# A convolution branch normalised in another place: standardise per token, scale and shift per channel on ACT, result kept in SBUF

## The chip, the core and the metric

One Trainium2 chip, and one of its cores. The kernel is a single program for the five engines of that core: PE (TensorE: matmuls and transposes), DVE (VectorE), ACT (ScalarE), POOL (GpSimd) and SP, whose queue issues most of the DMAs. The metric is device time in microseconds (us): the median of several runs of the whole program. A measurement of this kernel can tell about 0.2%, some 5 us, from no change.

## What is computed

One layer of a decoder with two kinds of heads, in float32, for 2048 tokens of width 1024. The part that matters here is the convolution group, one half of the mixer:

```python
def _layernorm(x, g, b):
    mu = jnp.mean(xf, axis=-1, keepdims=True)
    var = jnp.mean(jnp.square(xf - mu), axis=-1, keepdims=True)
    y = (xf - mu) * lax.rsqrt(var + EPS)
    return (y * g + b)

def _conformer_conv(val, gate, conv_w, conv_b, ln_g, ln_b):
    glu = val * jax.nn.sigmoid(gate)
    y = depthwise causal convolution of glu, width 31, 512 channels
    y = y + conv_b
    y = _layernorm(y, ln_g, ln_b)          # over the 512 channels of a token
    return jax.nn.silu(y)
...
a = _rmsnorm(h, g_pre_mix);  u = a @ w_in            # value, gate, q, k, v
attn_out = _rmsnorm(_stick_breaking(q, k, v), attn_norm_g)
y = concat(conv_out, attn_out) @ w_out
h = h + _rmsnorm(y, g_post_mix)
f = silu(_rmsnorm(h) @ w_gate) * (_rmsnorm(h) @ w_up) @ w_down
h = h + _rmsnorm(f, g_post_ffn)
```

## The kernel before

**Precision and layout.** Every dense product is done in three matmuls on numbers split into a high and a low part (H by a copy on ACT, L by a subtraction on DVE or POOL). Tokens go in four groups g of 512 (`G`), each of four tiles t of 128; 512 channels are four blocks c of 128. The convolution works with channels on the partitions and tokens along the free axis.

**Stages.** The mixer comes first: for each group the input projection (`inproj`), the taps of the convolution (`taps`), its normalisation (`convnorm`), attention in 128-query blocks (`attn`), and the output projection in two halves, `mixed`/`outproj` with part 0 for the convolution's channels and part 1 for attention's. The feed-forward follows, with seven products instead of eight per pair of blocks; its first piece, `c11`, and a second, `p4`, are run beside the last attention. PE alternates between these dense products and the small ones of attention.

**The convolution.** `taps(g)` accumulates 31 taps per channel block in the PSUM bank `cv`, one DVE instruction each (L817, L821), the last of which writes to `acc` in SBUF (one buffer). The bank `cv` exists once and serves, in the order in which it is asked for, the taps of the four blocks and then the transposes of `convnorm`; so the taps of group g+1 begin only when `convnorm(g)` has given it up.

**The normalisation.** `convnorm(g)` goes tile by tile. PE turns the tile to tokens on the partitions (`lps`, L834), ACT copies it to SBUF (L836), DVE makes mean and variance (L838, L840), POOL the inverse root (`rstd_of`, L537 and L538), DVE subtracts the mean and multiplies by the gain in one instruction and multiplies by the inverse root and adds the shift in another (L842, L843; gain `lng` and shift `lnb` are held broadcast over the partitions, 128x512 each), ACT makes the sigmoid (L845), POOL the product (L846), PE turns it back (`cps`, L851), ACT copies it (L853), and ACT's queue stores it to a scratch tensor `conv[g]` in DRAM (L854). Later `mixed(g, 0)` loads it block by block from SP's queue (L869) and splits it (L871, L872).

**What sets the order.** The mixer is first written down by generators that are advanced beside each other by the table `PLAN`. The instructions so recorded become a graph (`Graph`) with a cost of each instruction, buffers and links; `arrange` schedules it forwards and backwards several times and keeps the best, and `in_order` ties the instructions of each engine to that order. Any change of an instruction, a buffer or a dependency in the mixer may therefore move all the others. The feed-forward's order is pinned by hand, but for a few of its first instructions that may stand among the mixer's last. Tiles of `acc`, `cy`, `cs`, `lng`, `lnb` and others are used again as working space of the feed-forward (list `free`).

The steps of attention that are named later: `scores` makes z on PE (L908, L909), masks it on DVE (L911), takes two sigmoids on ACT (`om` L914, `A` L916), a running product on DVE (the scan, L918) and a product on POOL (`A`, L919); `values` turns A on PE (`at`, L935), splits it on ACT and DVE (`TH` L594, `TL` L595) and multiplies it with V (L940, L941). There are 320 scans in the mixer, and each engine's order can be counted by them.

## Time and profile before

| | |
|---|---|
| median of three runs | 2469.27 us (2466.63 to 2470.15) |
| the profiled execution | 2463.68 us, its span 2461.8 us |
| granted clock of PE | 0.993 of full speed |
| busy share PE, DVE, ACT, POOL | 96%, 73%, 52%, 62% |
| DMA | 657 MB, 267 GB/s on average |

The span is the time from the first to the last instruction of the profiled execution; its own time is 1.9 us longer. A row of a stretch gives, for each engine, busy time and number of instructions in it. "PEld" are the weight loads of PE, which overlap its matmuls. A matmul's record (about 390 ns for 512 columns) overlaps the next one's, so a stretch in which PE is "busy" all the time may still hold more matmuls than another. Instructions of DVE and ACT overlap a little as well.

### The profile page before, as it was taken

What the parts mean: (1) busy time and instruction counts of PE and PEld (TensorE: products, weight loads), DVE (VectorE), ACT (ScalarE), POOL (GpSimd) and SP (SyncE); (2) the same over time, 40 slices, a digit from 0 to 9 for tenths busy, and PEclk for the clock granted to TensorE, in tenths of its full rate; (3) what the DMA queues carried; (4) which work ended last, traced back from release to release, by engine and by line L of the source; (5) the groups of instructions that cost most, each with busy time, mean ns of one, the idle gap of its engine ahead of it and who ended that gap; (6) DMA issues with size and microseconds to landing.
All of it is one profiled execution on the core that took longest, in us unless ns stands there. A gap on an engine that the chain in (4) does not pass through costs nothing. (4 is left out here: it accounts for less than half of the span.)

```text
span 2461.8 us, 35571 instructions
## 1 busy us (share of the span) xinstructions
PE 2366.0 (96%) x11156; PEld 1927.0 (78%) x11156; DVE 1805.2 (73%) x2321; ACT 1290.2 (52%) x2398; POOL 1533.3 (62%) x1845
## 2 busy tenths in 40 slices
PE   8999999998999999999889998999999999999998
PEld 6788877786787878877678777787788887888886
DVE  6997999999997579998742247767665664557556
ACT  4557675685666566566654554333322334454543
POOL 5765567674667577659961138755656665568656
PEclk9999999999999999999999999999999999999999
DMA  9989876997689899976689768987878778658765
GB/s 324 290 304 287 259 235 218 300 310 250 226 263 307 277 330 325 324 261 202 201 299 312 252 256 294 319 280 257 295 273 291 258 246 282 196 190 273 248 190 178
DMA packets 289180, 657.31 MB, mean 267 GB/s; under 512 B 33888, under 2 KB 42080, under 8 KB 288992
## 3 DMA queue, kind: packets, MB, share of 16 engines
q1 hardware_dynamic: 264704, 622.01, 75.5%
q10 hardware_dynamic: 24288, 33.04, 3.7%
q8 instruction: 88, 1.44, 0.2%
q14 instruction: 100, 0.82, 0.1%
HBM read 460.92 MB, written 193.99 MB: 266 GB/s over the span
## 5 line engine op out<-in xcount | busy, mean ns | idle before, releaser
L919 POOL TENSOR_TENSOR A<-A,om 128x512 f32<-128x512 f32 (+2 forms) x320 | 326.2, 1021 | 286.1 <-DVE om L918 223.2
L1402 POOL TENSOR_TENSOR wL<-raw,wH 128x512 fp32r<-128x512 f32 x176 | 253.6, 1464 | 199.1 <-ACT wH L1401 168.2
L821 DVE SCALAR_TENSOR_TENSOR cv<-glu,cw,cv 128x512 f32<-128x512 f32 x464 | 345.7, 745 | 5.0
L1633 DVE TENSOR_TENSOR xL__22010<-t__22012,xH__22009 128x512 fp32r<-128x512 f32 x154 | 199.7, 1302 | 156.7 <-ACT xH__22009 L1632 155.1
L1631 POOL TENSOR_TENSOR xL__22008<-t__22011,xH__22007 128x512 fp32r<-128x512 f32 x154 | 211.4, 1380 | 153.2 <-ACT xH__22007 L1630 149.3
L918 DVE TENSOR_TENSOR_SCAN om<-om,one,z 128x513 f32<-128x513 f32 (+3 forms) x256 | 277.7, 1096 | 24.2 <-ACT A L916 21.9
L595 DVE TENSOR_TENSOR TL<-at,TH 128x512 fp32r<-128x512 f32 (+1 forms) x320 | 188.8, 600 | 105.5 <-ACT TH L594 79.2
L602 PE MATMUL inps<-xH,wL 128*128 128x512 f32 x640 | 257.8, 404 | 5.7 <-ACT sg L769 4.6
L606 PE MATMUL inps<-xL,wH 128*128 128x512 f32 x640 | 255.6, 400 | 0.0
L604 PE MATMUL inps<-xH,wH 128*128 128x512 f32 x640 | 254.4, 398 | 0.0
L914 ACT ACTIVATE om<-z 128x512 f32<-128x512 f32 (+2 forms) x320 | 173.7, 545 | 134.6 <-DVE z L911 67.5
L1108 PE MATMUL dps<-xH__22007,xL__22010 128*128 128x512 f32 x616 | 240.1, 390 | 2.5 <-DVE xL__22010 L1633 2.3
L1108 PE MATMUL dps<-xL__22008,xH__22009 128*128 128x512 f32 x616 | 240.1, 390 | 1.1 <-POOL xL__22008 L1631 1.0
L1108 PE MATMUL dps<-xH__22007,xH__22009 128*128 128x512 f32 x616 | 239.7, 389 | 0.0
L594 ACT ACTIVATE TH<-at 128x512 fp32r<-128x512 f32 (+1 forms) x320 | 169.3, 545 | 93.9 <-PE at L935 83.7
L935 PE MATMUL at<-idr,A 128*128 128x128 f32 x1088 | 200.7, 275 | 18.0 <-POOL A L919 9.4
L556 ACT ACTIVATE wH<-raw 128x1024 fp32r<-128x1024 f32 x156 | 166.3, 1066 | 89.2 <-PE inps L606 33.8
L1630 ACT ACTIVATE xH__22007<-t__22011 128x512 fp32r<-128x512 f32 x154 | 97.3, 632 | 214.7 <-POOL xL__22008 L1631 118.5
L1401 ACT ACTIVATE wH<-raw 128x512 fp32r<-128x512 f32 x176 | 101.2, 623 | 176.3 <-PE b L1108 53.2
L935 PEld LDWEIGHTS at<-idr,A 128*128 128x128 f32 x1088 | 140.6, 141 | 63.4 <-POOL A L919 16.0
L916 ACT ACTIVATE A<-z 128x512 f32<-128x512 f32 (+2 forms) x320 | 174.4, 549 | 4.3 <-PE at L935 3.6
L560 POOL TENSOR_TENSOR wL<-raw,wH 128x1024 fp32r<-128x1024 f32 x50 | 120.4, 2409 | 47.8 <-ACT wH L556 47.1
(304 smaller groups left out, 6347.9 us busy)
## 6 DMA issues: line engine op xcount, KB each, us to landing
wL<-wL SPq DMA_DIRECT2D x156, 512.0 KB, 5.5
raw<-in_w_in_dram SPq DMA_DIRECT2D x80, 512.0 KB, 5.7
t__22012<-u SPq DMA_DIRECT2D x154, 256.0 KB, 2.8
c<-c ACTq DMA_DIRECT2D x88, 256.0 KB, 5.7
t__22011<-wd SPq DMA_DIRECT2D x88, 256.0 KB, 2.9
K<-kd SPq DMA_DIRECT2D x80, 256.0 KB, 4.5
V<-vd SPq DMA_DIRECT2D x80, 256.0 KB, 4.6
u<-accf SPq DMA_DIRECT2D x22, 768.0 KB, 4.8
```

The lines of the kernel that those rows point to most:

```text
L595: nc.vector.tensor_tensor(L, ps, H.bitcast(F32), ALU.subtract)
L602: nc.tensor.matmul(ps, WL[:, kc], aH[t](k), start=k == 0, stop=False)
L604: nc.tensor.matmul(ps, WH[:, kc], aH[t](k), start=False, stop=False)
L606: nc.tensor.matmul(ps, WH[:, kc], aL[t](k), start=False, stop=k == KT - 1)
L821: nc.vector.scalar_tensor_tensor(to, gl[c][:, k:k + G], cw[:, c, k:k + 1], a, ALU.mult, ALU.add)
L918: nc.vector.tensor_tensor_scan(r, r, (one if late else z[:, 0:1]).to_broadcast([P, w + 1]), one, ALU.mult, ALU.bypass)
L919: nc.gpsimd.tensor_tensor(a[:, 0:w], a[:, 0:w], om[:, G - w + 1:G + 1], ALU.mult)
L935: nc.tensor.transpose(pt[:, j * P:(j + 1) * P], u["A"][j][:, b * P:(b + 1) * P], id32)
L1108: return nc.tensor.matmul(ps, a, b, skip_group_check=True, **flags)
L1402: nc.gpsimd.tensor_tensor(l, t, f32(h), sub)
L1631: nc.gpsimd.tensor_tensor(WL, w, f32(WH), sub)
L1633: nc.vector.tensor_tensor(UL, t, f32(UH), sub)
```

## The change

The gain and shift of the normalisation are moved from the turned tile, where they lie along the free axis, behind the second transpose, where they lie along the partitions.

- Per tile: ACT's copy of the turned tile goes back into the tile's own place in `acc`; the statistics read PSUM; one DVE instruction subtracts the mean and multiplies by the inverse root, in place.
- When the four tiles are done, per channel block: PE turns the 512 tokens back into the bank `cv`; ACT makes the sigmoid of scale x + shift into a rotating buffer (`ev`), and scale x + shift itself (Identity) into `acc`, with gain and shift as operands per partition; POOL multiplies the two in place.
- `acc` has two buffers and is handed to `mixed(g, 0)` as it is. The scratch tensor, its 16 stores from ACT's queue and its 16 loads from SP's queue are gone, as are `cy`, `cs` and the broadcast `lng` and `lnb`; the four small vectors (bias, attention's gain, gain, shift) are in one tile, the last two loaded in pieces of four bytes.
- The pauses between the steps (`LAG` times `yield 3` per tile) are half as long and stand behind each tile and each block.
- The working space of the feed-forward uses the second `acc` in place of the removed tiles.

```diff
-    lng = const(cc, "lng", ln_g.partition_broadcast(P), [P, CH])
-    lnb = const(cc, "lnb", ln_b.partition_broadcast(P), [P, CH])
-    ag = const(cc, "ag", attn_g, [P, CB])
+    small4 = cc.tile([P, 4, CB], F32, name="small4")
+    cb_, ag, lng, lnb = (small4[:, i, :] for i in range(4))
+    waiting += [(cb_, conv_b), (ag, attn_g)]
+    waiting += [(v, w.rearrange("(c p) -> p c", p=P)) for v, w in ((lng, ln_g), (lnb, ln_b))]
...
-        acc = vp.tile([P, CB, G], F32, tag="acc", name="acc", bufs=1)
-        conv[g] = dp.tile([P, CB, G], F32, name=f"conv{g}")
+        acc = conv[g] = vp.tile([P, CB, G], F32, tag="acc", name="acc", bufs=2)
...
-            ps = pp.tile([P, G], F32, tag="cv", name="lps", bufs=1)
+            ps = pp.tile([P, G], F32, tag="cv", name="lps", bufs=1).rearrange("p (c t) -> p c t", c=CB)
             for c in range(CB):
-                nc.tensor.transpose(ps[:, c * P:(c + 1) * P], acc[:, c, ts_], id32)
-            y = vp.tile([P, CH], F32, tag="cy", name="cy", bufs=1)
+                nc.tensor.transpose(ps[:, c, :], acc[:, c, ts_], id32)
+            y = acc[:, :, ts_]
             nc.scalar.activation(y, ps, AF.Copy)
             st = sp.tile([P, 6], F32, tag="st", name="st")
-            nc.vector.bn_stats(st, y)
+            nc.vector.bn_stats(st, ps.rearrange("p c t -> p (c t)"))
             mv = sp.tile([P, 3], F32, tag="mv", name="mv")
             nc.vector.bn_aggr(mv[:, 0:2], st)
             rstd_of(mv[:, 2:3], mv[:, 1:2], 1, "msc", 2)
-            nc.vector.scalar_tensor_tensor(y, y, mv[:, 0:1], lng, ALU.subtract, ALU.mult)
-            nc.vector.scalar_tensor_tensor(y, y, mv[:, 2:3], lnb, ALU.mult, ALU.add)
-            s = vp.tile([P, CH], F32, tag="cs", name="cs", bufs=1)
-            nc.scalar.activation(s, y, AF.Sigmoid)
-            nc.gpsimd.tensor_tensor(s, y, s, ALU.mult)
-            for _ in range(LAG):
+            nc.vector.tensor_scalar(y, y, mv[:, 0:1], mv[:, 2:3], ALU.subtract, ALU.mult)
+            for _ in range(LAG // 2):
                 yield 3
-            pt = pp.tile([P, G], F32, tag="cv", name="cps", bufs=1).rearrange("p (c t) -> p c t", c=CB)
-            for c in range(CB):
-                nc.tensor.transpose(pt[:, c, :], s[:, c * P:(c + 1) * P], id32)
-            r = s.rearrange("p (c t) -> p c t", c=CB)
-            nc.scalar.activation(r, pt, AF.Copy)
-            nc.scalar.dma_start(conv[g][:, :, ts_], r)
+        for c in range(CB):
+            ps = pp.tile([P, G], F32, tag="cv", name="cps", bufs=1)
+            for t in range(TT):
+                nc.tensor.transpose(ps[:, t * P:(t + 1) * P], acc[:, c, t * P:(t + 1) * P], id32)
+            s = ev("silu")
+            nc.scalar.activation(s, ps, AF.Sigmoid, scale=lng[:, c:c + 1], bias=lnb[:, c:c + 1])
+            nc.scalar.activation(acc[:, c, :], ps, AF.Identity, scale=lng[:, c:c + 1], bias=lnb[:, c:c + 1])
+            nc.gpsimd.tensor_tensor(acc[:, c, :], acc[:, c, :], s, ALU.mult)
+            for _ in range(LAG // 2):
+                yield 3
...
-        ms = [ma[g, p] if part else ev("m") for p in range(CB)]
-        if not part:
-            for k in range(CB):
-                nc.sync.dma_start(ms[k], conv[g][:, k, :])
+        ms = [ma[g, p] if part else conv[g][:, p, :] for p in range(CB)]
...
-        free = [t[:, 0:G] for t in gl] + [vp.tile([P, CH], F32, tag=n, name=n, bufs=1) for n in ("cy", "cs")]
-        acc = vp.tile([P, CB, G], F32, tag="acc", name="accf", bufs=1)
+        acc3, more = (vp.tile([P, CB, G], F32, tag="acc", name="accf", bufs=2) for _ in range(2))
```

The order of the mixer is made anew, and nearly every row of it moves. Three places matter. Lines behind L809 are numbered one to four lower after the change (L918 is L914, L821 is L820, L838 is L837).

DVE at the normalisation of group 1, before: the first of its four tiles, among scans (`om`) of attention.

```order
L838 BN_STATS st<-cy 128x6
L918 SCALAR_TENSOR_TENSOR om<-om,one,z 128x129
L840 BN_AGGR mv<-st 128x2
L918 SCALAR_TENSOR_TENSOR om<-om,one,z 128x257
L842 SCALAR_TENSOR_TENSOR cy<-cy,mv,lng 128x512
L911 TENSOR_TENSOR z<-z,msk 128x128 x2
L843 SCALAR_TENSOR_TENSOR cy<-cy,mv,lnb 128x512
```

The same place after:

```order
L837 BN_STATS st<-lps 128x6
L774 TENSOR_TENSOR glu_136<-inps,sg 128x512
L839 BN_AGGR mv<-st 128x2
L914 SCALAR_TENSOR_TENSOR om<-om,one,z 128x513
L841 TENSOR_SCALAR acc<-acc,mv 128x4x128
L837 BN_STATS st<-lps 128x6
```

The four tiles now stand within five scans of each other (behind scans 100 to 105), where they stood behind scans 96 to 123, and one instruction of 512 columns stands for two.

DVE at the first taps of group 3, before (`TL` is attention's split, `ot` and `ss` its own normalisation); 232 scans stand ahead of L817:

```order
L918 SCALAR_TENSOR_TENSOR om<-om,one,z 128x513
L963 TENSOR_REDUCE ss_11901<-sq 128x8
L817 TENSOR_SCALAR cv<-glu_137,cw,cbias 128x512
L595 TENSOR_TENSOR TL<-at,TH 128x256
L821 SCALAR_TENSOR_TENSOR cv<-glu_137,cw,cv 128x512
L918 SCALAR_TENSOR_TENSOR om<-om,one,z 128x513
```

After; 202 scans stand ahead of L816:

```order
L914 SCALAR_TENSOR_TENSOR om<-om,one,z 128x513
L816 TENSOR_SCALAR cv<-glu_134,cw,small_121 128x512
L820 SCALAR_TENSOR_TENSOR cv<-glu_134,cw,cv 128x512
L595 TENSOR_TENSOR TL<-at,TH 128x512
L914 SCALAR_TENSOR_TENSOR om<-om,one,z 128x513
L820 SCALAR_TENSOR_TENSOR cv<-glu_134,cw,cv 128x512 x2
```

The taps of group 3 begin 30 scans earlier; those of group 1 begin behind scan 48 instead of 50, those of group 2 behind scan 112 instead of 128.

ACT at the feed-forward's first Silu (`accf<-a`, L1416; `c` are the evictions of c11, L1149), before:

```order
L836 ACTIVATE cy<-lps 128x512
L1416 ACT_TABLE_LOAD
L1416 ACTIVATE accf<-a_17364 128x512
L594 ACTIVATE TH<-at 128x512
L916 ACT_TABLE_LOAD
L916 ACTIVATE A<-z 128x512
```

After:

```order
L1412 ACT_TABLE_LOAD
L1412 ACTIVATE accf<-a_17276 128x512
L1145 ACTIVATE c_15372<-c_15392 128x512
L1110 DMA c_2_1_0_0_15449<-c_15372 128x512
L556 ACTIVATE wH<-raw 128x1024
L1145 ACTIVATE c_15372<-c_15391 128x512
```

The Silu stands behind scan 309 of attention on ACT, where it stood behind scan 316; the load of the sigmoid's table that must follow it stands 13 rows further on. The feed-forward behind the mixer has the same rows in the same order as before on every engine.

More of the change, by code (lines that the diff above doesn't have):

```diff
@@ L631, in layer_kernel @@
     cw = const(cc, "cw", conv_w, [P, CB, CW])
-    cb_ = const(cc, "cbias", conv_b, [P, CB])
-    lng = const(cc, "lng", ln_g.partition_broadcast(P), [P, CH])
-    lnb = const(cc, "lnb", ln_b.partition_broadcast(P), [P, CH])
-    ag = const(cc, "ag", attn_g, [P, CB])
+    small4 = cc.tile([P, 4, CB], F32, name="small4")
+    cb_, ag, lng, lnb = (small4[:, i, :] for i in range(4))
+    waiting += [(cb_, conv_b), (ag, attn_g)]
+    waiting += [(v, w.rearrange("(c p) -> p c", p=P)) for v, w in ((lng, ln_g), (lnb, ln_b))]
     gpf = const(cc, "gpf", g_pre_ffn, [P, KT])
@@ L1352, in layer_kernel @@
         mixer.arrange()
-        free = [t[:, 0:G] for t in gl] + [vp.tile([P, CH], F32, tag=n, name=n, bufs=1) for n in ("cy", "cs")]
-        acc = vp.tile([P, CB, G], F32, tag="acc", name="accf", bufs=1)
-        sums3, us = acc[:, 0:3, :], four(acc)[0:3]
-        free += [acc[:, 3, :]]
+        acc3, more = (vp.tile([P, CB, G], F32, tag="acc", name="accf", bufs=2) for _ in range(2))
+        acc, more = four(acc3), four(more)
+        sums3, us = acc3[:, 0:3, :], acc[0:3]
+        free = [t[:, 0:G] for t in gl] + more[0:2] + [acc[3]]
         free += [fup.tile([P, G], F32, tag="rb", name="rbf")]
         free += [fup.tile([P, G], F32, tag="sum", name="sumf", bufs=3) for _ in range(3)]
-        free += [lng, lnb]
+        free += more[2:4]
         s1_, u_ = cycle(free[0:2]), cycle(free[3:6])
```

## The prediction

> **What bounds the kernel now.** I read the page first (busy time by engine), then the busy time of each engine by stretches of the span, then the waits inside the stretches in which TensorE (PE) loses time, and last the rows of the lines that the change touches.
>
> ```profile
> span 2461.8 us, 35571 instructions
> PE 2366.0 (96%) x11156; PEld 1927.0 (78%) x11156; DVE 1805.2 (73%) x2321; ACT 1290.2 (52%) x2398; POOL 1533.3 (62%) x1845
> ...
> core 0: us, PE busy (x) PEld busy (x) DVE busy (x) ACT busy (x) POOL busy (x), PEclk, DMA share, GB/s
> 180.00:250.00 70.00, 69.95 (x380) 57.53 (x379) 53.13 (x87) 50.72 (x102) 40.76 (x87) 1.00 0.91 289
> 250.00:460.00 210.00, 199.93 (x1004) 162.86 (x1004) 206.44 (x304) 126.69 (x245) 131.70 (x206) 1.00 0.76 248
> 460.00:540.00 80.00, 79.64 (x429) 64.40 (x428) 73.18 (x106) 66.87 (x138) 64.72 (x127) 1.00 0.92 302
> 540.00:740.00 200.00, 190.62 (x931) 150.82 (x931) 196.87 (x289) 119.53 (x227) 116.95 (x201) 0.99 0.77 250
> 740.00:940.00 200.00, 196.97 (x1018) 160.84 (x1017) 143.29 (x190) 133.09 (x253) 142.01 (x216) 1.00 0.91 307
> 940.00:1140.00 200.00, 195.26 (x947) 159.45 (x946) 192.07 (x252) 119.98 (x221) 131.49 (x173) 0.99 0.83 285
> 1140.00:1310.00 170.00, 152.28 (x738) 121.80 (x737) 98.15 (x116) 105.58 (x200) 129.94 (x169) 0.96 0.74 253
> 1460.00:2461.00 1001.00, 968.24 (x4252) 794.39 (x4250) 646.42 (x676) 394.67 (x716) 644.01 (x479) 1.00 0.75 253
> 2250.00:2430.00 180.00, 179.87 (x794) 148.55 (x793) 108.59 (x93) 87.87 (x165) 113.22 (x86) 1.00 0.71 228
> ```
>
> PE is busy for 96% of the span, so nothing can be won but PE's idle time, and that lies unevenly. In 250 to 460 us PE loses 210 - 199.9 = 10.1 us and in 540 to 740 us 9.4 us, and in both VectorE (DVE) is busy for 98% (206.4 of 210, 196.9 of 200). These are the stretches in which DVE runs the convolution's taps of groups 1 and 2 beside attention. Between them, in 460 to 540 us, where group 1 is normalised, DVE has 6.8 us free and PE loses 0.4 us. In 740 to 940 us, while group 2 is normalised, DVE has 57 us free; the taps of group 3 follow in 940 to 1140 us (DVE 96%, PE loses 4.7 us). From 1460 us on the feed-forward runs; the order of its instructions is unchanged on every engine. So I look at the mixer, and there at DVE.
>
> ```profile
> PE z L908 <- DVE om L918: 6.3, 10, 1.1
> PE ops L1034 <- DVE big L1039: 3.7, 2, 3.3
> PE o L941 <- DVE TL L595: 3.0, 6, 1.0
> PE o L940 <- ACT TH L594: 2.4, 4, 0.9
> ```
>
> These are PE's waits in 250 to 760 us (total, times, longest): 13.0 us of the longest four end on DVE, 2.4 us on ACT. DVE's queue is in order, so whatever leaves it lets the scans and splits that PE waits for come sooner.
>
> **What the change takes from DVE.** The rows have count, busy time and mean of one in ns:
>
> ```profile
> L843 DVE SCALAR_TENSOR_TENSOR cy<-cy,mv,lnb 128x512 f32<-128x512 f32 x16 | 16.8, 1052 | 8.9 <-POOL mv L538 8.9
> L842 DVE SCALAR_TENSOR_TENSOR cy<-cy,mv,lng 128x512 f32<-128x512 f32 x16 | 15.0, 937 | 0.3
> L838 DVE BATCH_NORM_STATS2 st<-cy 128x6 f32<-128x512 f32 x16 | 10.9, 684 | 0.6 <-ACT cy L836 0.6
> L719 DVE TENSOR_SCALAR hrow<-hrow,rstd 128x1024 f32<-128x1024 f32 x12 | 9.9, 821 | 1.8 <-POOL rstd L538 1.8
> L817 DVE TENSOR_SCALAR cv<-glu,cw,cbias 128x512 f32<-128x512 f32 x16 | 12.9, 806 | 0.3
> ```
>
> For each of the 16 token tiles two scalar_tensor_tensor go (937 + 1052 = 1989 ns) and one tensor_scalar of 128x512 comes. No row has it in this shape. Upwards it is bounded by L817, 806 ns (two scalars per partition, but into PSUM); downwards by half of L719, 410 ns (SBUF to SBUF, one scalar, twice as wide). I take 450 ns, near the second, because source and target are both in SBUF as there. The statistics read PSUM instead of SBUF; I leave them at 684 ns. So a tile gives DVE 1989 - 450 = 1.54 us (bounds 1.18 and 1.58), a group of four tiles 6.2 us, all sixteen 24.6 us. Only what falls in or next to the two full stretches counts.
>
> *Group 1 (540 to 740 us).* Its four tiles stand at 460 to 540 us. The 6.2 us saved there and the 6.8 us that DVE has free there are 13.0 us into which taps of group 2 can move up. By the order they do: the first tap of group 2 stands behind scan 112 of attention on DVE, and stood behind scan 128.
>
> ```profile
> 0.00:500.00 500.00, 112.00 (x112) 1.00 0.85 277
> 0.00:820.00 820.00, 211.86 (x200) 1.00 0.84 276
> 0.00:962.00 962.00, 259.19 (x241) 1.00 0.85 281
> ```
>
> (Scans L918 begun so far; the number behind x counts them.) Scan 112 comes at 500 us. With 13.0 us less, DVE is at 184 of 200 us in this stretch and no longer full, and PE's 190.6 us of work become the limit: at most 9.4 us. What PE still loses beside a DVE at 92 to 96% lies between 0.4 us in 80 us (460 to 540 us, that is 1.0 in 200) and 4.7 us in 200, so the gain is 4.7 to 8.4 us. I take 6.5 us; the ends are 0 (if PE is held by something else) and 9.4 us.
>
> *Group 0 (250 to 460 us).* Its four tiles stand at 190 to 250 us, where DVE is not full (53 of 70 us) and PE loses nothing. The saving helps the full stretch behind only as far as taps of group 1 begin earlier: they stand behind scan 48 instead of 50, two scans, some 3 us of DVE work. I take 3 us, between 0 and the 6.2 us saved.
>
> *Group 2 (740 to 1140 us).* Its own saving is worth nothing: DVE has 57 us free there, which cover it. But its chain is shorter (below), so the taps of group 3 begin behind scan 202 instead of 232, at about 820 us. By scan 240 some 70 more taps have been issued than before, 70 x 0.745 = 52 us of DVE work moved from the stretch behind 940 us to the one ahead of it.
>
> ```profile
> L821 DVE SCALAR_TENSOR_TENSOR cv<-glu,cw,cv 128x512 f32<-128x512 f32 x464 | 345.7, 745 | 5.0
> ```
>
> PE loses 3.0 + 4.7 = 7.7 us in the two stretches now. In 740 to 962 us, where scan 240 began, DVE had 143.3 + 0.96 x 22 = 164 us of work; with 52 more and 6.2 saved it is 210 of 222 us, 95%, between the 92% of 460 to 540 us (1.0 lost in 200) and the 96% of 940 to 1140 us (4.7 in 200): some 4 us lost. The 178 us behind it are left with DVE at about 67%, as in 740 to 940 us (3.0 in 200): 2.7 us lost. So 6.8 instead of 7.7 us; I take 1 us of gain. The ends are a gain of 4.7 us, and the loss that the second rival prices.
>
> *Group 3.* Its tiles stand behind 1180 us, where DVE is at 58% or less. Nothing.
>
> **What the change does on ACT, POOL, PE and the queues.**
>
> ```profile
> L845 ACT ACTIVATE cs<-cy 128x512 f32<-128x512 f32 x16 | 10.4, 649 | 5.4 <-DVE cy L843 3.8 <-DMA conv<-cs 1.6
> L836 ACT ACTIVATE cy<-lps 128x512 f32<-128x512 f32 x16 | 9.9, 620 | 7.7 <-PE lps L834 7.6
> L853 ACT ACTIVATE cs<-cps 128x512 f32<-128x512 f32 x16 | 9.8, 614 | 1.6 <-PE cps L851 0.9 <-POOL pv L921 0.6
> L975 ACT ACTIVATE ma<-po,ag 128x512 f32<-128x512 f32 x16 | 11.0, 689 | 5.4 <-PE po L973 5.4
> L854 ACTq DMA_DIRECT2D conv<-cs x16: 520/521/587, 205.3 to 1381.0; - x16
> L869 SPq DMA_DIRECT2D m<-conv x16: 371/440/1519, 339.5 to 1393.0; - x16
> conv<-cs ACTq DMA_DIRECT2D x16, 256.0 KB, 6.4
> m<-conv SPq DMA_DIRECT2D x16, 256.0 KB, 5.7
> ```
>
> ACT keeps three ACTIVATEs per tile, but two of them now take scale and bias per partition. One such operand costs 689 - 614 = 75 ns (L975 against L853), so two make 764 ns; 620 + 2 x 764 = 2148 ns stand for 649 + 620 + 614 = 1883 ns, 4.2 us more in all. Against that ACT no longer issues 16 stores (16 x 0.52 = 8.3 us of its queue) and SP no longer issues 16 loads (16 x 0.44 = 7.0 us). ACT gains 4 us, which is worth nothing where it is 60% busy. The 8 MB of traffic (of 657 MB) and the two landings of 6.4 and 5.7 us leave the way from the convolution to its projection; the first store is issued at 205 us and the first load at 339 us, and for the last group PE had c11 to do meanwhile, so that cover makes it worth nothing too. POOL keeps its 16 products and PE its 128 transposes: no change.
>
> The Trainium skill speaks against this placement: its page "ScalarE: Activation LUTs", section "Rules for kernel authors", sends multiply and add to VectorE, not to ScalarE. By that rule scale and shift would cost DVE another 806 ns (L817) per channel block, the saving per group would fall from 6.2 to 3.0 us, and the sum to about half. The stretches above decide against the rule here: DVE is 98% busy where ACT is at 60%.
>
> The chain of waits through the one PSUM bank `cv` gets shorter. Before, each tile went through transpose, copy, statistics, POOL, two DVE steps, sigmoid, POOL and back, eight steps in line, before the next tile had the bank; now the bank is free when copy and statistics have read it (0.62 and 0.68 us). The bank then goes to the four channel blocks, each held for two ACTIVATEs (1.5 us). That, not the DVE time alone, lets the next taps start 16 and 30 scans earlier.
>
> At the start, two loads of 256 KB (gain and shift, broadcast) become two of 2 KB in pieces of four bytes. Nearest rows:
>
> ```profile
> L513 SPq DMA_DIRECT2D cbias<-in_conv_b_dram x1: 708/708/708, 4.7 to 4.7; - x1
> L513 SPq DMA_DIRECT2D lng<-in_conv_ln_g_dram x1: 328/328/328, 7.6 to 7.6; - x1
> ```
>
> With four times as many pieces as cbias each takes SP between 0.33 and 4 x 0.71 = 2.8 us; behind them stands the third weight load. I take 0, ends -0.5 and +2 us.
>
> Last, the feed-forward's first Silu moves. It had to wait for the single `acc`; with two it takes group 2's and stands on ACT behind scan 309 instead of 316, among the first evictions of the second half of c11.
>
> ```profile
> 1370.13 1.28 ACT L1416 ACT_TABLE_LOAD   x1
> ...
> 1372.57 1.28 ACT L916 ACT_TABLE_LOAD   x1
> ...
> 1378.53 0.50 PE L1108 MATMUL c<-xH,wL 128*128 128x512 f32 x1 [2.35 <-ACT c L1149]
> ...
> L1462 SPq DMA_DIRECT2D a<-c x2: 319/372/426, 1268.5 to 1274.9; - x2
> ...
> DMA to landing us min/median/max: 5.8/6.5/7.1
> ```
>
> The two table loads (1.28 us each) remain. Behind them PE waited 2.35 us; at the new place ACT could also wait for the Silu's operand, whose load was issued at 1268.5 us and takes 6.5 us. I take 0 (the same stall elsewhere), ends -2.4 and +6 us.
>
> **Sum.** -6.5 - 3 - 1 + 0 + 0 = -10.5 us. The profiled execution took 2463.68 us (span 2461.8 and 1.9 us around it), so 2453.2 us, 0.43% less. The three runs have a median of 2469.27 us, 0.23% above that execution; 0.43% off the median is 2459 us. Differences under 0.2% (4.9 us) a measurement of this kernel can hardly tell from none.
>
> **Rivals.**
>
> *More than that.* If PE's real room is larger than its idle time, DVE's relief is the limit: 6.2 + 13.0 us. The weight loads (PEld) speak for it: where PE runs without a gap, in 2250 to 2430 us, they are busy 148.55 of 180 us, 82.5%; in the two full stretches 77.6% and 75.4%, which leaves 210 - 162.86/0.825 = 12.6 and 17.2 us, not 10.1 and 9.4. Then -20 us, about 2449 us. Against it: attention's chains and the two PSUM banks of the projections also hold PE. The Trainium skill says the same of the measure ("Perfetto Trace Analysis", section "Identifying the Most-Contended Engine": judge TensorE by LDWEIGHTS busy, not by matmul busy); the trace agrees, as these shares show.
>
> *The gain is given back.* The taps pulled ahead fill DVE from 740 us on. Should DVE be as full over 740 to 1040 us as it was in 540 to 740 us, PE loses 9.4/200 x 300 = 14.1 us there instead of 3.0 + 2.4 = 5.4, that is +8.7 us, and the sum is -9.5 + 8.7 = -0.8 us: 2468 us, no difference. For it: the 95% worked out above are not far from 98%. Against it: at 96% PE lost half as much. It decides at a DVE share of 98% in that stretch.
>
> *Slower.* ACT stops at the Silu behind scan 309: its operand's load shares SP's queue with weight loads that wait for their own buffers. While ACT stands, c11 can fill two banks of 12 matmuls (24 x 0.227 = 5.4 us, by the 794 in 180 us of 2250 to 2430 us), then PE stops, and attention with it. A stall of S costs S + 2.6 - 5.4 - 2.4; to turn -10.5 us into a loss of 5 us it must be 21 us. Against it: that load took 6.5 us. At S = 25 us the time is about 2474 us.
>
> **How the numbers follow.** The forecast 0.50, more 0.14, given back 0.22, slower 0.14. Faster is the first two, 0.64. The forecast's own range is 2454 to 2464 us. To leave out no more than two in ten I reach to 2447 us (most of the second case) and to 2473 us (the third whole, the slower one in part).
>
> **What would show it.** Right: DVE below 95% and PE's loss below 4 us in 540 to 740 us; the taps of group 3 from about 820 us; tensor_scalar near 0.45 us; the span from 1460 us on, counted from the projection's end, unchanged. Wrong: DVE at 98% in 740 to 1040 us; a gap on PE of more than 5 us behind an ACT_TABLE_LOAD; tensor_scalar at 0.8 us; or new PE waits in 1140 to 1310 us, where it loses 17.7 us already and where the order has moved as well.

## The result, and the profile after

| | before | after |
|---|---|---|
| median of 4 runs, us | 2469.71 (2466.63 to 2471.67) | 2448.31 (2442.64 to 2451.81) |
| profiled execution, us (span) | 2463.68 (2461.8) | 2447.04 (2445.3) |

The ratio is 0.9911, 95% interval 0.9893 to 0.9930: the changed kernel is 0.89% faster, some 22 us. The direction is as forecast and the time lies inside the range, but the gain is twice the 0.43% that the sum gave. The two profiled executions differ by 16.6 us. They ran at the same granted clock of PE, 0.993; the four executions of the changed kernel had 0.992 to 0.994, those of the kernel before 0.986 to 0.994 in the experiments below, 0.990 on average. In the last set its executions at 0.986 to 0.988 took 2470.4 to 2473.1 us, and those at 0.992 and 0.993 took 2463.2 to 2466.5 us, some 7 us for 0.005; by this estimate some 4 us of the 22 go with the clock, and why the two kernels get different ones stays open.

First the page's line of busy time by engine, and the stretches of the changed kernel (per stretch: length, then busy time with count of PE, PEld, DVE, ACT, POOL, the granted clock, DMA share, GB/s):

```profile
span 2445.3 us, 35497 instructions
...
PE 2360.7 (97%) x11156; PEld 1927.7 (79%) x11156; DVE 1786.1 (73%) x2305; ACT 1295.6 (53%) x2398; POOL 1528.3 (62%) x1845
```
```profile
250.00:460.00 210.00, 208.00 (x1052) 171.36 (x1051) 207.45 (x315) 132.23 (x255) 135.69 (x218) 1.00 0.79 254
460.00:540.00 80.00, 77.33 (x410) 62.67 (x409) 76.62 (x110) 67.08 (x133) 61.16 (x123) 0.98 0.87 287
540.00:740.00 200.00, 195.46 (x972) 157.50 (x972) 196.24 (x286) 126.44 (x239) 125.66 (x216) 0.99 0.78 255
740.00:940.00 200.00, 194.34 (x1000) 157.76 (x999) 173.68 (x238) 130.36 (x244) 134.87 (x205) 1.00 0.91 308
940.00:1140.00 200.00, 194.04 (x942) 157.06 (x940) 151.47 (x190) 123.44 (x229) 136.34 (x175) 1.00 0.80 267
1140.00:1310.00 170.00, 153.65 (x753) 123.61 (x752) 95.50 (x110) 104.32 (x193) 118.58 (x160) 0.98 0.75 256
```

In 250 to 460 us PE loses 2.0 us where it lost 10.1, in 540 to 740 us 4.5 instead of 9.4. In both, DVE is as full as before (207.45 of 210, 196.24 of 200). In 740 to 1140 us PE loses more than before, 11.6 instead of 7.8 us. All in all the span is 16.5 us shorter. PE's idle time fell from 95.8 to 84.6 us (span less busy), that is 11.2 of it; the other 5.3 us are busy time of the same 11156 matmuls (2366.0 to 2360.7), which the forecast did not count at all. In the last 1001.8 us of the span PE is busy for 968.2 us before and 968.3 us after: the feed-forward is unchanged, as forecast.

DVE is full and PE runs: what changed is what DVE is full of. The taps' line alone in 540 to 740 us, before and then after:

```profile
540.00:740.00 200.00, 87.43 (x119) 0.99 0.77 250
```
```profile
540.00:740.00 200.00, 75.75 (x102) 0.99 0.78 255
```

The 124 operations of a group's taps took from 537 to 740 us, nearly the whole stretch; now they go from 490 to 726 us. In this stretch that is 17 taps and 11.7 us fewer. Attention's scans, splits (`TL`) and masks got only 2.7 us of the place, the first tiles of group 2's normalisation 3.2 us, and projections and smaller pieces the rest; but what PE waits for comes sooner. The waits of PE in 250 to 760 us (total, times, longest) show it: the four longest rows were 15.4 us together, and are 6.5 us now.

```profile
PE z L904 <- DVE om L914: 3.0, 3, 1.7
PE ops L1030 <- DVE xL L868: 1.3, 1, 1.3
PE po L969 <- DVE ot L961: 1.3, 1, 1.3
PE o L936 <- ACT TH L594: 0.9, 2, 0.8
```

The rows of the lines that are new (min/median/max ns, first and last start):

```profile
L841 DVE TENSOR_SCALAR acc<-acc,mv x16: 515/548/1623, 194.7 to 1220.7; 128x512 f32<-128x512 f32 x16
L837 DVE BATCH_NORM_STATS2 st<-lps x16: 667/696/700, 191.2 to 1213.9; 128x6 f32<-128x512 f32 x16
L849 ACT ACTIVATE silu<-cps,small x16: 774/820/869, 213.3 to 1383.6; 128x512 f32<-128x512 f32 x16
L850 ACT ACTIVATE acc<-cps,small x16: 779/819/876, 214.0 to 1384.3; 128x512 f32<-128x512 f32 x16
```

### The profile page after: what moved, and what is told of

Read it like the earlier page. It is cut to its first block, busy times and chain, and to the rows that moved or that the text cites. A ratio compares the mean times of both kernels' runs of the same rounds, so it can differ in the third digit from the quotient of the medians.

```text
span 2445.3 us, 35497 instructions
## 1 busy us (share of the span) xinstructions
PE 2360.7 (97%) x11156; PEld 1927.7 (79%) x11156; DVE 1786.1 (73%) x2305; ACT 1295.6 (53%) x2398; POOL 1528.3 (62%) x1845
## 5 line engine op out<-in xcount | busy, mean ns | idle before, releaser
L820 DVE SCALAR_TENSOR_TENSOR cv<-glu,cw,cv 128x512 f32<-128x512 f32 x464 | 346.8, 747 | 4.7
L914 DVE TENSOR_TENSOR_SCAN om<-om,one,z 128x513 f32<-128x513 f32 (+3 forms) x256 | 278.3, 1100 | 16.6 <-ACT A L912 13.6
L931 PEld LDWEIGHTS at<-idr,A 128*128 128x128 f32 x1088 | 140.1, 140 | 58.2 <-POOL A L915 16.5
```

The costliest lines, as they stand in the source:

```text
L820: nc.vector.scalar_tensor_tensor(to, gl[c][:, k:k + G], cw[:, c, k:k + 1], a, ALU.mult, ALU.add)
L914: nc.vector.tensor_tensor_scan(r, r, (one if late else z[:, 0:1]).to_broadcast([P, w + 1]), one, ALU.mult, ALU.bypass)
L931: nc.tensor.transpose(pt[:, j * P:(j + 1) * P], u["A"][j][:, b * P:(b + 1) * P], id32)
```

## The experiments

Eighteen kernels, each timed in five rounds against the kernel before. The theories: **D**, DVE's work that leaves is the gain (the forecast's step). **P** (called C or "the chain" in the expectations), the new path through the bank `cv` (statistics from the bank, all four tiles first, then the four channel blocks, two `acc` tiles) is the gain, by an earlier and more even start of the next taps. **M**, the round trip through DRAM. **O**, the planner, given other work, happened to find a better order. In the edits, lines are cut to what differs.

### First set: putting single parts back

**dve_back**

```diff
-nc.vector.tensor_scalar(y, y, mv[:, 0:1], mv[:, 2:3], ALU.subtract, ALU.mult)
+nc.vector.scalar_tensor_tensor(y, y, mv[:, 0:1], idb, ALU.subtract, ALU.mult)
+nc.vector.scalar_tensor_tensor(y, y, mv[:, 2:3], idb, ALU.mult, ALU.add)
```

> The changed kernel with the two DVE instructions per tile put back: two scalar_tensor_tensor of 128x512 with a constant tile as second operand stand for the one tensor_scalar; the values are therefore not the normalised ones. The rest (statistics from PSUM, bank cv given back early, result kept in SBUF) is as in the changed kernel. Theory D (the gain is DVE work that left the two full stretches): the 1.4 us per tile come back, 6 us before the taps of group 1 and 6 before those of group 2, 2460 to 2466 us. Theory C (the gain is the shorter chain through the bank cv, which lets taps begin earlier): 2448 to 2453 us. Theory M (the DRAM round trip) and theory O (the order is new and happens to be good): no statement that tells them apart here.

Measured: 2454.69 us (2453.35 to 2456.67), ratio 0.9944 (0.9932 to 0.9956). DVE has all its old work again, and two thirds of the gain stay: D is not the whole gain.

**dve_less**, the other side, in the kernel before:

```diff
-nc.vector.scalar_tensor_tensor(y, y, mv[:, 0:1], lng, ALU.subtract, ALU.mult)
-nc.vector.scalar_tensor_tensor(y, y, mv[:, 2:3], lnb, ALU.mult, ALU.add)
+nc.vector.tensor_scalar(y, y, mv[:, 0:1], mv[:, 2:3], ALU.subtract, ALU.mult)
```

> The kernel before with only its two scalar_tensor_tensor per tile replaced by one tensor_scalar (subtract the mean, multiply by the inverse root); gain and shift are left out, all else (tile by tile through the bank cv, store to DRAM and load) is as before. Theory D: most of the gain, 2451 to 2458 us. Theory C: next to none, 2464 to 2470 us. Theory M: none, 2466 to 2471 us.

Measured: 2472.64 us (2467.59 to 2483.88), ratio 1.0021 (1.0007 to 1.0034). With the old path and in this order, the relief of DVE gains nothing: in the full stretches DVE is a little emptier (206.4 and 196.9 us before), but the weight loads, PE's work, are as before (162.86 and 150.82 us). The relief was smaller than meant, too: the sixteen tensor_scalar took 960 ns on average. And the granted clock is lower in this execution (0.99 and 0.97 here, 1.00 and 0.99 before).

```profile
250.00:460.00 210.00, 202.44 (x1000) 162.84 (x999) 200.49 (x296) 129.09 (x246) 141.16 (x213) 0.99 0.77 252
540.00:740.00 200.00, 193.20 (x925) 151.82 (x923) 194.00 (x283) 121.40 (x226) 120.47 (x200) 0.97 0.80 252
```

**dram_back**

```diff
+nc.scalar.dma_start(conv[g][:, c, :], acc[:, c, :])
-ms = [ma[g, p] if part else conv[g][:, p, :] for p in range(CB)]
+ms = [ma[g, p] if part else ev("m") for p in range(CB)]
+nc.sync.dma_start(ms[k], conv[g][:, k, :])      # four per group
```

> The changed kernel with the round trip put back: ACT's queue stores each finished channel block to DRAM (16 stores of 256 KB) and SP's queue loads it ahead of the split (16 loads). Theory M (8 MB of traffic, 16 issues on ACT's and 16 on SP's queue, and the two landings were worth something): 2453 to 2460 us. Theories D and C: 2447 to 2451 us, as the changed kernel.

Measured: 2455.54 us (2452.51 to 2458.05), ratio 0.9946 (0.9934 to 0.9958).

**after_hop**, the changed kernel with `HOP = 63.0` in place of `60.0`, a cost that only the planner uses:

> The changed kernel with one number of the planner's cost model changed (the hop after a wait 63 for 60 ns): same instructions, another order of the mixer. Theory O: the order alone moves the time by 5 us and more, anywhere from 2440 to 2460 us. Theories D, C and M: within 4 us of the changed kernel, 2444 to 2452 us.

Measured: 2450.55 us (2445.76 to 2455.14), ratio 0.9931 (0.9918 to 0.9944).

### Second set: both parts back, and the old order of tiles

**both_back** is dve_back and dram_back together.

> The changed kernel with the two scalar_tensor_tensor per token tile on DVE and the round trip of the convolution's result through DRAM both put back (the constant tile of the second steps makes the normalised values wrong); the path of the tiles through the bank cv is the changed kernel's. The first taps of groups 2 and 3 stand behind scans 107 and 202. If DVE's work or the traffic carries the gain, nothing of it is left: 2466 to 2471 us. If the shorter path through the bank, which lets the taps begin earlier, carries it: faster than the kernel before by 7 to 13 us, 2456 to 2462 us. If it is only a lucky order of the changed kernel (scatter of the planner), anything from 2455 to 2475 us.

Measured: 2460.54 us (2455.48 to 2466.71), ratio 0.9973 (0.9962 to 0.9984). All of the old DVE work and the old round trip, on the new path: still 7 us faster than before.

**tile_by_tile**

```diff
+            for _ in range(LAG):
+                yield 3
+            pt = (bank cv) ... four transposes of this tile
+            nc.scalar.activation(s, pt, AF.Sigmoid, ...); Identity; product on POOL
-        for c in range(CB): ...        # the loop over channel blocks
```

> The changed kernel (one tensor_scalar per tile, result stays in SBUF) but each token tile goes through the bank cv to the end before the next one enters, as in the kernel before; scale and shift take channel block 0's operands for all blocks (left out: the right gain and shift of blocks 1 to 3). The first taps of groups 2 and 3 stand behind scans 116 and 205, near the changed kernel's 112 and 202. If the early start of the taps carries the gain: 2448 to 2455 us. If it is the order by channel blocks itself (four long holds instead of four tiles): 2460 us or more. DVE's work and the traffic, as theories of their own, say 2448 us too, so this run tells only about the order by blocks.

Measured: 2459.40 us (2451.94 to 2461.59), ratio 0.9962 (0.9948 to 0.9976). About half of the gain is left, in one order of this work. The edit also puts the pause per tile back to its old length.

**before_lag3** is the kernel before with `LAG = 3`.

> The kernel before with LAG = 3 instead of 4 (the planner's pause between the two transposes of a tile), and nothing else: same instructions, same DVE work, same DRAM round trip. The first taps of groups 2 and 3 move up from scans 128 and 232 to 118 and 218. If an early start of the taps carries the gain: 2459 to 2464 us, some two thirds of the way in scans giving about half of the gain. If DVE's work or the traffic carries it: within 2 us of the kernel before, 2467 to 2472 us. If the planner's orders scatter by more than that: no theory is helped.

Measured: 2469.41 us (2461.83 to 2473.44), ratio 1.0011 (0.9998 to 1.0023): no gain. Its stretches 540 to 740 and 1140 to 1310 us:

```profile
540.00:740.00 200.00, 193.06 (x953) 154.13 (x952) 197.38 (x283) 127.45 (x241) 122.05 (x211) 0.99 0.78 258
1140.00:1310.00 170.00, 145.65 (x699) 114.44 (x697) 99.96 (x106) 99.82 (x190) 129.12 (x162) 0.96 0.71 240
```

The earlier taps do what P says where they run (PE loses 6.9 us instead of 9.4), and the later stretch takes it back (24.3 us instead of 17.7). An early start is not enough by itself.

**before_hop** is the kernel before with `HOP = 63.0`.

> The kernel before with the planner's cost HOP = 63 instead of 60, which only shuffles the order; the first taps of groups 2 and 3 stand behind scans 129 and 228 (128 and 232 before), the two table loads behind scan 309 instead of 316. It measures how far an order by itself moves the time. Scatter as with the same edit in the changed kernel (+2 us): 2466 to 2473 us. If the early place of the Silu is worth anything it shows here as a gain or loss over that.

Measured: 2461.97 us (2458.90 to 2467.26), ratio 0.9981 (0.9971 to 0.9990). An order alone is worth up to 5 us, so no single kernel with an order of its own decides anything smaller.

### Third set: the order held still

Here the planner's result is kept, instruction by instruction on every engine, and only work is added or taken away.

**before_light**, with the order of before written in as a table:

```diff
-nc.vector.scalar_tensor_tensor(y, y, mv[:, 0:1], lng, ALU.subtract, ALU.mult)
-nc.vector.scalar_tensor_tensor(y, y, mv[:, 2:3], lnb, ALU.mult, ALU.add)
+nc.vector.tensor_scalar(y, y, mv[:, 0:1], mv[:, 2:3], ALU.subtract, ALU.mult)
+nc.vector.scalar_tensor_tensor(y[:, 0:1], y[:, 0:1], mv[:, 2:3], lnb[:, 0:1], ALU.mult, ALU.add)
```

> The kernel before with its order kept instruction by instruction (the planner's result is written in as a table), and DVE relieved: the first scalar_tensor_tensor of a tile becomes the change's tensor_scalar, the second touches one column instead of 512 (left out: gain and shift). Some 1.35 us less on DVE per tile, 21.6 us in all, nothing moved. If DVE's work itself carries the gain, most of the 7 us that it cost to put it back in the changed kernel: 2461 to 2464 us. If the order that the planner finds carries it: 2467 to 2470 us. It also tells whether the earlier run with a cheap normalisation, which came out no faster, was spoiled by its own order.

Measured: 2464.91 us (2459.89 to 2475.89), ratio 0.9985 (0.9971 to 0.9998): 4 us. The interval all but reaches to no change. (Its profiled execution was 11 us above its median, so no row of it is used.)

**after_heavy**, in the order of the changed kernel:

```diff
 nc.vector.bn_aggr(mv[:, 0:2], st)
+nc.vector.bn_stats(st, idb)      # twice
```

> The changed kernel with its order kept instruction by instruction, and two more bn_stats of 128x512 from SBUF behind each tile's bn_aggr on DVE (their result is used by nothing): 2 x 0.68 = 1.37 us more per tile, 21.9 us in all, as much DVE work as the kernel before has. If DVE's work itself carries the gain: 2454 to 2457 us, as with the two scalar_tensor_tensor put back. If the order carries it: 2448 to 2450 us.

Measured: 2461.17 us (2455.05 to 2461.91), ratio 0.9961 (0.9946 to 0.9977): 0.0050 more than the changed kernel's 0.9911, 12 us for 22 us of DVE.

**quick_bank**

```diff
-nc.scalar.activation(s, ps, AF.Sigmoid, scale=lng[:, c:c + 1], bias=lnb[:, c:c + 1])
 nc.scalar.activation(acc[:, c, :], ps, AF.Identity, scale=lng[:, c:c + 1], bias=lnb[:, c:c + 1])
+nc.scalar.activation(s, acc[:, c, :], AF.Sigmoid)
```

> The changed kernel with the Identity first, from the bank cv into SBUF, and the Sigmoid behind it from SBUF: the bank is free after one ACTIVATE (0.8 us) instead of two (1.6 us) per channel block, the result is the same. If the path through the bank carries the gain, it gets shorter by 3 us per group: 2443 to 2447 us. If not: 2447 to 2452 us (the planner finds another order, which scatters by some 5 us).

Measured: 2456.14 us (2454.80 to 2457.23), ratio 0.9945 (0.9929 to 0.9960). Slower than the changed kernel by 0.34%, though the bank is free earlier. An order of the same work (dram_order) differs by 0.32%, so this doesn't tell what the shorter hold is worth.

**after_rate** is the changed kernel with the planner's `RATE = 345.0`.

> The changed kernel with the planner's rate of transfers at 345 instead of 350, which only shuffles the order. A third order of the same work, for the scatter: by the two known (2448 and 2451 us) 2446 to 2454 us. If the gain were a lucky order, it would be 2460 us or more.

Measured: 2451.30 us (2447.45 to 2452.68), ratio 0.9921 (0.9905 to 0.9938).

### Fourth set: which of order, queue and traffic

**dram_small**

```diff
-nc.scalar.dma_start(conv[g][:, c, :], acc[:, c, :])
+nc.scalar.dma_start(conv[g][:, c, 0:8], acc[:, c, 0:8])
-nc.sync.dma_start(ms[k], conv[g][:, k, :])
+nc.sync.dma_start(ms[k][:, 0:8], conv[g][:, k, 0:8])
+ms = [accs[g][:, p, :] for p in range(CB)]
```

> dram_back (2455.5 us) with its order kept instruction by instruction, its 16 stores and 16 loads still issued, but of 8 columns instead of 512; the projection reads the result from SBUF and waits for no load. If the 8 MB and the landings are what the round trip costs: 2448 to 2451 us. If it is the order, or the issue of the 32 transfers in the queues of ACT and SP: 2454 to 2457 us.

Measured: 2455.34 us (2454.18 to 2458.67), ratio 0.9949 (0.9937 to 0.9962).

**dram_order** is the changed kernel itself with the order of dram_back written in as a table, its 32 transfers struck out.

> The changed kernel in the order that the planner found for the run with the DRAM round trip put back, with its 32 transfers struck out: same instructions as the changed kernel, other order. If the issue of the 32 transfers (16 x 0.5 us of ACT's queue, 16 x 0.4 us of SP's) costs the 7 us: 2448 to 2451 us. If it is the order: 2454 to 2457 us.

Measured: 2454.01 us (2450.78 to 2457.77), ratio 0.9943 (0.9927 to 0.9959). The stretch 540 to 740 us of dram_back, dram_small and dram_order in turn:

```profile
540.00:740.00 200.00, 193.74 (x974) 156.41 (x972) 197.65 (x285) 131.25 (x247) 129.86 (x221) 1.00 0.82 267
```
```profile
540.00:740.00 200.00, 193.68 (x971) 156.32 (x970) 198.04 (x285) 130.88 (x247) 129.09 (x221) 1.00 0.80 261
```
```profile
540.00:740.00 200.00, 193.52 (x970) 155.88 (x969) 198.09 (x284) 130.47 (x247) 128.51 (x219) 1.00 0.78 258
```

The traffic falls (267, 261, 258 GB/s) and PE does the same. M falls wholly: at a held order, 8 MB, 32 issues and 32 landings cost less than a measurement can tell. The 6 to 7 us between the medians of these and of the changed kernel are the order.

**after_late**, in the order of the changed kernel:

```diff
 nc.vector.scalar_tensor_tensor(to, gl[c][:, k:k + G], cw[:, c, k:k + 1], a, ALU.mult, ALU.add)
+if g and c == 0 and 8 <= k < 16:
+    nc.vector.bn_stats(ones[:, 2:8], idb)
```

> The changed kernel with its order kept, and eight more bn_stats of 128x512 on DVE (8 x 0.68 = 5.5 us) among the taps 8 to 15 of the first channel block of groups 1, 2 and 3, 16.4 us in all, away from the chain of the normalisation. DVE's work: some 0.6 us for each us in the stretches of groups 1 and 2 as in the run with the work beside bn_aggr (13 us for 22), half of it for group 3: 2455 to 2458 us. The chain: nothing, 2448 to 2451 us.

Measured: 2460.52 us (2456.33 to 2463.80), ratio 0.9967 (0.9954 to 0.9980): 0.0056 more than the changed kernel, 14 us for 16.5 us of DVE, away from the normalisation, though among taps, which hold the bank too.

**before_heavy**, in the order of before, with the same two bn_stats as in after_heavy:

> The kernel before with its order kept and two more bn_stats of 128x512 behind each tile's bn_aggr on DVE, 21.9 us in all. If DVE's work costs the same in the order of before as in the changed one (13 us for 22): 2480 to 2484 us. If the order of before hides it, as taking work away (4 us for 21.6) lets one think: 2472 to 2475 us. The chain: each tile holds the bank 1.4 us longer, so it too gives 2475 to 2485 us; the two theories part only over before_light.

Measured: 2478.27 us (2477.76 to 2482.08), ratio 1.0044 (1.0032 to 1.0057): 11 us for 22 us of DVE.

**ident_act**

```diff
-nc.scalar.activation(y, ps, AF.Copy)
-nc.vector.tensor_scalar(y, y, mv[:, 0:1], mv[:, 2:3], ALU.subtract, ALU.mult)
+nc.gpsimd.tensor_scalar(mv[:, 3:4], mv[:, 0:1], mv[:, 2:3], -1.0, ALU.mult, ALU.mult)
+nc.scalar.activation(y, ps, AF.Identity, scale=mv[:, 2:3], bias=mv[:, 3:4])
```

> The changed kernel, normalised on ACT: an Identity with rstd as scale and -mean*rstd as bias, from the bank into SBUF, takes the place of the copy on ACT and of the tensor_scalar on DVE (one small product more on POOL); same result. DVE loses 16 x 0.55 = 8.8 us of work, the bank is held some 2 us longer per tile (until mean and rstd are there). DVE's work: 2443 to 2447 us. The chain through the bank: slower than the changed kernel, 2452 to 2458 us.

Measured: 2454.19 us (2451.29 to 2456.16), ratio 0.9940 (0.9928 to 0.9953). DVE loses its sixteen tensor_scalar (13.5 us by their rows), and the kernel gains nothing by it; the longer hold of the bank would explain it, and so would the scatter of orders. Neither this nor quick_bank beats the changed kernel, and with a shorter and a longer hold of the bank the two come out alike (0.9945 and 0.9940).

**before_rate** is the kernel before with `RATE = 345.0`.

> The kernel before with the planner's rate of transfers at 345 instead of 350, which only shuffles the order. The orders of this kernel so far gave 2469 and 2464 us (and 2471 us with a shorter pause): 2463 to 2473 us. At 2455 us or less the gain of the change would be within the scatter of orders.

Measured: 2469.80 us (2466.00 to 2473.21), ratio 1.0006 (0.9996 to 1.0015).

### What they say together

At held orders, the start of attention's scans (number 49, 97, 129, 201, 241, 305 on DVE; us from the span's start) shows where added DVE work costs time:

```
               49     97    129    201    241     305
after         254.7  452.5  530.0  806.6  962.9  1241.5
after_heavy   257.0  458.2  541.0  821.9  977.6  1256.1
after_late    255.4  458.7  539.1  816.0  975.8  1255.0
before        253.8  464.9  537.9  822.6  962.0  1256.1
before_heavy  255.8  468.0  546.0  836.3  975.8  1266.5
```

after_heavy's lag behind the changed kernel grows by 5.7 us up to scan 97 (group 0's four tiles brought 5.6 us of added work), by 5.3 up to 129 (group 1's), by 4.3 up to 201 (group 2's), and by nothing behind it. So in the first three groups a microsecond of DVE is nearly a microsecond of the kernel, and in the last none. That is the forecast's picture for groups 1 and 3. For group 2, whose saving the forecast put at nothing, it is not, nor is it in the order of before: before_heavy's lag grows by 5.7 us between scans 129 and 241 (8.1 to 13.8), over its group 2. Each row is one execution, and scans compare only kernels of the same order.

And the four combinations of path and DVE work, as mean of the ratios over the orders that were run of each:

| | DVE's old work | DVE relieved |
|---|---|---|
| old path | 1.0000 (1.0000, 0.9981, 1.0006, 1.0011) | 1.0003 (1.0021, 0.9985) |
| new path | 0.9958 (0.9944, 0.9973) | 0.9927 (0.9911, 0.9931, 0.9921, 0.9943) |

(Old path, old work: the kernel before, before_hop, before_rate, before_lag3; new path, relieved: the changed kernel, after_hop, after_rate, dram_order. The orders of one cell spread by 0.29 to 0.36%, so a mean over two to four of them is good to 0.1 or 0.2%.) The new path with the old work is worth 0.4%, 10 us. The relief is worth another 0.3%, 8 us, on the new path (quick_bank and ident_act, variants that are not in the cell, would make it 0.26%), and nothing that shows on the old one; that DVE's work does count on the new path is shown apart from the scatter by the held orders. On the old path the held orders say that it counts too when it is added (before_heavy, 11 us for 22 us) and hardly when it is taken away (before_light, 4 us for an intended 21.6), so that the old path can't use relief is not shown. Over its orders the change gains 0.7%, 18 us; the order that it happens to have is the best of four, worth another 4 us.

Why the path counts is shown as far as this: in 540 to 740 us PE loses 6.8 to 11.7 us in the six kernels on the old path (without before_light) and 2.1 to 6.9 us in the thirteen on the new one, while DVE is 97 to 99.5% busy in all of them. The two ranges touch, and over the whole of 250 to 1310 us they overlap (38 to 51 us and 35 to 44 us): part of what is won here is lost again behind it. The first taps of group 2 stand behind scans 118 to 129 in the former and 106 to 116 in the latter. Two rows at the ends, before_rate and dve_back:

```profile
540.00:740.00 200.00, 188.35 (x898) 148.03 (x897) 196.73 (x278) 122.62 (x232) 126.06 (x208) 0.97 0.77 249
```
```profile
540.00:740.00 200.00, 197.88 (x1008) 161.49 (x1007) 197.13 (x291) 129.52 (x244) 123.12 (x217) 1.00 0.79 256
```

What stays open: which part of the path does it. Kernels on the new path also have two `acc` tiles and take the statistics straight from the bank; tile_by_tile, which has these but neither the order by blocks nor the halved pauses, keeps about half, in a single order of its own. No run gives the kernel before a second `acc` alone. That the time for which the bank is held is what counts, no run shows. And why the old path gets so little from a relieved DVE is argued (its taps can't move up while the bank is held), not shown.

## Why the prediction was right or wrong, point by point

*The step that failed.* The sum gave -10.5 us and some 21 us came. Only DVE's time has a price other than nothing in it: the shorter path through the bank, which the forecast itself names as what lets the next taps start earlier, has no term, and its scan counts enter only as room on DVE. By the table above the path is worth about 10 us, the relief about 8, and this order 4 more than the mean of its four. The cause inside the path stays open.

*DVE holds PE in the full stretches: right*, but not there alone (group 2 below). At a held order, 22 us of work back on DVE cost 12 us, and 16.5 us away from the normalisation cost 14 us; in the order of before, 22 us cost 11 us.

*Group 1, -6.5 us by emptying DVE below 95%: wrong mechanism.* DVE stayed at 98%, the forecast's own sign of failure, and PE's loss still fell, from 9.4 to 4.5 us. That this lies inside the forecast's 4.7 to 8.4 us of gain, at its lower end, is luck. What failed here is the subtraction "DVE is at 184 of 200 us in this stretch": what the taps leave free is filled with other work (11.7 us of taps fewer, 0.6 us of DVE fewer), so here the share of busy time did not tell whether the waiting scan comes soon. That the taps start 16 scans earlier was read rightly from the order:

```profile
0.00:490.00 490.00, 112.59 (x112) 1.00 0.84 277
0.00:810.00 810.00, 214.88 (x202) 1.00 0.84 276
```

Scan 112 had begun at 490 us and scan 202 at 810 us, so groups 2 and 3 begin where the text said. But the shorter path got no price of its own. It stands in the forecast as a sentence ("That, not the DVE time alone, ..."), and the 10 us of the table are about the size of what is missing.

*Group 0, -3 us: too small.* In 250 to 460 us PE loses 8.1 us less in this profile, more than the "6.2 us saved" that was the term's bound. The order alone moves this number by as much: before_hop and before_rate lose 4.7 and 4.6 us here with the old work, where the kernel before loses 10.1, and dram_order 8.7 us with the new, where the changed kernel loses 2.0. So how much of the 8.1 us is DVE's saving stays open.

*Group 2, -1 us: wrong in sign.* PE loses 3.8 us more in 740 to 1140 us (5.7 and 6.0 us in its halves). The rival "given back" had the direction but not the mechanism: DVE is at 87% and 76% there, not 98%, and in 740 to 962 us at 88% where 95% had been worked out. PE's longest waits in this stretch are now these, 0.9 and 0.8 us before:

```profile
PE z L904 <- DVE om L914: 4.0, 8, 0.9
PE at L931 <- POOL A L915: 3.5, 4, 2.3
```

"Its own saving is worth nothing" is not borne out either: at held orders 5.6 us of work added beside group 2's tiles cost 4.3 us in the order of the changed kernel and 5.7 us in that of the kernel before, though DVE is not full there (87% and 72% in 740 to 940 us).

*DVE's saving, 1.54 us per tile: too high.* The tensor_scalar took 548 ns at the median and 845 on average (13.5 us over 16; six of them were held up, see the last section), so the saving is 1.14 us a tile, below the lower bound of 1.18. DVE's busy time fell by 19.1 us, not 24.6.

*ACT: right.* The two ACTIVATEs take 0.82 us where 0.764 stood, and ACT is 63% busy in 540 to 740 us. The Trainium skill's page "ScalarE: Activation LUTs", section "Rules for kernel authors", was set aside for this. No run moves scale and shift to DVE; dve_back, which leaves them on ACT and only adds to DVE, is 0.33% slower than the changed kernel. *The DRAM round trip, worth nothing: right*, and shown by dram_order. *The start: right*, nothing lost there.

*The Silu: right in time, wrong in its reason.* It stands behind scan 309. ACT stood still for 4.70 us ahead of its table load, which the profile puts down to the landing of a weight load, and PE then waited for one of ACT's evictions of c11:

```profile
1257.48 1.28 ACT L1412 ACT_TABLE_LOAD   x1 [4.70 <-DMA raw<-in_w_gate_dram]
```
```profile
PE c L1104 <- ACT c L1145: 3.2, 1, 3.2
```

That wait of 3.2 us is the only one of its kind in the stretch (the mixer of before had 2.35 us behind its second load). But before_hop, with a single `acc`, has the Silu behind scan 309 too, so the second tile was not needed for that place.

*The rivals.* "More than that" (about 2449 us) gave the time. Its premise, that the weight loads measure PE's real room, is borne out where it was drawn from: they rose from 162.86 to 171.36 us in 250 to 460 us, 81.6% of it, close to the 82.5% of a stretch without gaps, and PE's idle time alone accounts for 11.2 of the 16.5 us. Its cause, DVE's relief alone, is not: with DVE's old work on the new path two thirds of the gain stay. A stall of 21 us behind the Silu did not come. (The 2474 us of that rival do not add up: a stall of 25 us gives +9.3 us, that is 2473 us from the profiled execution and 2479 us from the median.)

*The size.* A scatter of 0.3% over orders of the same work was nowhere in the range's working. It is as large as most terms of the sum.

## What to carry to other kernels

A full engine that works through an in-order queue with several customers is better judged by which instruction a customer waits for than by its share: here it stayed at 98% while PE's loss in that stretch halved. Where work and order change together, hold the order still and change the work, and shuffle the order with the work held: the first showed the DRAM round trip to be worth nothing and DVE nearly 1 to 1 in the right places, the second that an order by itself is worth 5 to 8 us. And price a shorter path through a single buffer as a term of its own, beside the work that it saves.

## What was not expected of the hardware

The tensor_scalar of 128x512 took 515 to 549 ns in ten of its sixteen executions and 0.88 to 1.62 us in six. In those six a tensor_tensor of POOL was running when it began, or began within 60 ns of it, and it ended 280 to 287 ns behind the end of that product. A seventh, at 734.98 us, began while a product was running that ended 155 ns later, and took 537 ns. The first of them in the timeline (start, duration):

```profile
194.58 1.28 POOL L1188 TENSOR_TENSOR sum<-sum 128x512 f32<-128x512 f32 x1
194.65 1.49 DVE L841 TENSOR_SCALAR acc<-acc,mv 128x512 f32<-128x512 f32 x1 [1.49 <-POOL mv L538]
```

The product ends at 195.86 us, the tensor_scalar at 196.14. The Trainium skill's page "SBUF — State Buffer", section "SBUF: two separate sides", says that one port pair is shared by the two engines and that certain instructions of VectorE and those of GpSimd lock it: whichever starts first has it for its whole instruction, and the other blocks fully. Four of the six agree with it. In the other two POOL's product began 53 ns behind the tensor_scalar, by the records, and still went first; that is not explained here. Products of POOL that began over 110 ns behind it did not lengthen it.
